# Softmax mixture on one core: evictions that gather column halves into row pairs on two engines, 32 KB store rows, and last stores in two queues

## The chip, the core and the metric

The kernel runs on one core of a Trainium2 chip. TensorE (PE), VectorE (DVE), ScalarE (ACT) and GpSimd (POOL) each take their own instructions in order. SyncE (SP) and ScalarE issue the DMAs here. SP's go to the queue that the profile calls q1, ScalarE's to q10. All of them run on the core's 16 DMA engines. The metric is the device time of one execution in microseconds; less is better.

## What is computed

For each of 32 x 128 = 4096 rows there are four heads of 4096 logits and four prior logits. The result is the mean of the four softmaxes, weighted with the softmax of the priors:

```python
prior_probs = np.exp(prior - prior.max(axis=-1, keepdims=True))
prior_probs = prior_probs / prior_probs.sum(axis=-1, keepdims=True)
softmax = np.exp(logits - logits.max(axis=-1, keepdims=True))
softmax = softmax / softmax.sum(axis=-1, keepdims=True)
mixture = np.sum(prior_probs[..., None] * softmax, axis=2)   # [32, 128, 4096]
```

The logits are 268.4 MB of float32, read once; the result is 67.1 MB, written once.

## The kernel before

**Tiling.** The 4096 rows are cut into G = 32 groups of 128, and each group into J = 2 tiles of M = 64 rows; row 2m + j of a group is row m of its tile j. So there are N = 64 tiles. A tile lies in a slot of 128 partitions: partition 2m + q holds the heads 2q and 2q + 1 of row m, 32 KB in all. Index i (0 or 1) names the half of a slot, one head per partition, 4096 numbers. There are five slots, and `load(n)` fills one with a 4 MB DMA from SP (line 65; the last tile comes in two halves, line 68).

**Work on a tile.** `top(n, i)` takes the row maximum on VectorE (line 74) and the exponential on ScalarE, in place, with its sum beside it (line 77). `weigh(n, i)` takes the reciprocal of the sum (line 82, VectorE), makes from it and the prior a 128 x 64 weight matrix (line 84, GpSimd), and multiplies with it on TensorE (line 91): the matmul adds the two partitions of a row, and the second call (i = 1) adds the other two heads in PSUM. A tile's 64 x 4096 results stand in one PSUM tile `acc` of 128 x 2048: partitions 0 to 63 hold columns 0 to 2047 (c = 0), partitions 64 to 127 columns 2048 to 4095 (c = 1). [...]

**Eviction and store.** `evict(n)` is one ScalarE copy of 128 x 2048 out of `acc` (line 106) into the group's place in the output buffer `obuf`, which has room for two groups. `store(g)` writes a group with two DMAs of 1 MB (line 111), one per column half c: 64 partitions, two rows j each, 8 KB per row. For groups below HOLD = 28 they are issued from ScalarE, right behind the eviction. The last four groups are held back: groups 28 and 29 stay in `obuf`, groups 30 and 31 go into a slot that is no longer needed, and all of them are stored from SP, behind the last loads in SP's queue.

**Order.** The order is written by hand. Step n of the loop (lines 148 to 163) issues, with w = n - 1: `top(n, 0)`, `weigh(w, 1)`, `load(w + 5)`, `top(n, 1)`, `weigh(n, 0)`, `evict(w)` and, for the second tile of a group, its store. So on VectorE a step is maximum, reciprocal, maximum, reciprocal; on ScalarE it is exponential, exponential, eviction of the tile before, sometimes a store. After the loop the last tile is finished (lines 165 to 169). Semaphores between engines are put in by the layer that records the program, from the tiles that instructions read and write; an instruction that waits holds up all that stands behind it on its engine.

Of the kernel before, what the change touches and what calls it, by code (L numbers as in the profile page):

```python
# [1 line left out]

# [4 lines left out]

FP32 = mybir.dt.float32
AF = mybir.ActivationFunctionType
ALU = mybir.AluOpType  # L10
AX = mybir.AxisListType

P = 128
M = 64
J = 2
Q = 2
BANK = 512
SLOTS = 5


@with_exitstack
def kernel(
    ctx: ExitStack,
    tc: tile.TileContext,
    logits: bass.AP,
    prior: bass.AP,
    out: bass.AP,
):
    nc = tc.nc
    B, S, H, V = logits.shape  # L30
    R = M * J
    G = B * S // R
    N = G * J
    W = V // 2
    assert G * R == B * S and G == 32 and H == 2 * Q and V == 8 * BANK


    lg = logits.rearrange("b s h v -> (b s) h v").rearrange(
        "(g m j) (q i) v -> g j m q (i v)", m=M, j=J, i=Q
    )  # L40
    ov = out.rearrange("b s v -> (b s) v").rearrange("(g m j) v -> g m j v", m=M, j=J)
    pv = prior.rearrange("b s h -> (b s) h").rearrange("(g r) h -> g r h", r=R)

    cpool = ctx.enter_context(tc.tile_pool(name="cpool", bufs=1))
    psum = ctx.enter_context(tc.tile_pool(name="psum", bufs=1, space=bass.MemoryType.PSUM))

    slots = [cpool.tile([P, Q, V], FP32, name=f"slot{i}") for i in range(SLOTS)]

    obuf = cpool.tile([P, 2, J, W], FP32, name="obuf")
    accs = [psum.tile([P, W], FP32, name=f"acc{i}") for i in range(2)]  # L50

    sel = cpool.tile([P, M], FP32, name="sel")
    wts = [[cpool.tile([P, M], FP32, name=f"wt{k}{i}") for i in range(Q)] for k in range(2)]
    pr = cpool.tile([G, R, H], FP32, name="pr")
    pn = cpool.tile([G, J, Q, M, Q], FP32, name="pn")
    pmax = cpool.tile([G, R], FP32, name="pmax")
    pp = cpool.tile([P, J, Q, G], FP32, name="pp")
    nmax = [cpool.tile([P, N], FP32, name=f"nmax{i}") for i in range(Q)]
    dsum = [cpool.tile([P, N], FP32, name=f"dsum{i}") for i in range(Q)]
    rden = [cpool.tile([P, N], FP32, name=f"rden{i}") for i in range(Q)]  # L60

    def load(n):
        src = lg[n // J, n % J]
        if n < N - 1:
            nc.sync.dma_start(out=slots[n % SLOTS], in_=src)  # L65
        else:
            for i in range(Q):
                nc.sync.dma_start(
                    out=slots[n % SLOTS][:, i], in_=src[:, :, i * V : (i + 1) * V]
                )  # L70

    def top(n, i):
        x = slots[n % SLOTS][:, i]
        nc.vector.tensor_reduce(  # L74
            out=nmax[i][:, n : n + 1], in_=x, axis=AX.X, op=ALU.max, negate=True
        )
        nc.scalar.activation(  # L77
            x, x, AF.Exp, bias=nmax[i][:, n : n + 1], accum_out=dsum[i][:, n : n + 1]
        )

    def weigh(n, i):
        nc.vector.reciprocal(rden[i][:, n : n + 1], dsum[i][:, n : n + 1])  # L82
        wt = wts[n % 2][i]
        nc.gpsimd.tensor_scalar(  # L84
            out=wt, in0=sel, scalar1=rden[i][:, n : n + 1],
            scalar2=pp[:, n % J, i, n // J : n // J + 1], op0=ALU.mult, op1=ALU.mult,
        )

        for b in range(W // BANK):
            for c in range(2):  # L90
                nc.tensor.matmul(  # L91
                    accs[n % 2][c * M : (c + 1) * M, b * BANK : (b + 1) * BANK],
                    lhsT=wt,
                    rhs=slots[n % SLOTS][:, i, c * W + b * BANK : c * W + (b + 1) * BANK],
                    start=i == 0, stop=i == Q - 1,
                )

    HOLD = G - 4

    def home(g):  # L100
        if g < G - 2:
            return obuf[:, g % 2]
        return slots[(N - 5) % SLOTS][:, g % 2].rearrange("p (j w) -> p j w", j=J)

    def evict(n):
        nc.scalar.copy(home(n // J)[:, n % J], accs[n % 2])  # L106

    def store(g, js=slice(0, J)):
        eng = nc.scalar if g < HOLD else nc.sync
        for c in range(2):  # L110
            eng.dma_start(
                out=ov[g, :, js, c * W : (c + 1) * W], in_=home(g)[c * M : (c + 1) * M, js]
            )

    with tc.manual_schedule():
        for n in range(SLOTS):
            load(n)
        nc.scalar.dma_start(out=pr, in_=pv)

        nc.gpsimd.memset(sel, 1.0)  # L120
        nc.gpsimd.affine_select(  # L121
            out=sel, in_=sel, compare_op=ALU.is_ge, fill=0.0, base=0,
            pattern=[[-Q, M]], channel_multiplier=1,
        )
        nc.gpsimd.affine_select(  # L125
            out=sel, in_=sel, compare_op=ALU.is_ge, fill=0.0, base=Q - 1,
            pattern=[[Q, M]], channel_multiplier=-1,
        )

        nc.vector.reduce_max(pmax, pr, axis=AX.X)  # L130
        nc.vector.tensor_sub(pr, pr, pmax.unsqueeze(2).to_broadcast([G, R, H]))  # L131
        nc.scalar.activation(pr, pr, AF.Exp)  # L132
        nc.vector.reduce_sum(pmax, pr, axis=AX.X)  # L133
        nc.vector.reciprocal(pmax, pmax)  # L134
        prv = pr.rearrange("g (m j) (q i) -> g j i m q", j=J, i=Q)
        pmv = pmax.rearrange("g (m j) -> g j m", j=J)
        for j in range(J):
            for i in range(Q):
                nc.vector.tensor_mul(  # L139
                    pn[:, j, i], prv[:, j, i], pmv[:, j].unsqueeze(2).to_broadcast([G, M, Q])  # L140
                )
        pq = pn.rearrange("g j i m q -> g j i (m q)")
        for t in range(P // 32):
            nc.vector.transpose(  # L144
                pp[32 * t : 32 * (t + 1)], pq[:, :, :, 32 * t : 32 * (t + 1)]
            )

        for n in range(N):
            w = n - 1
            top(n, 0)  # L150
            if w >= 0:
                weigh(w, 1)
                if w + SLOTS < N:
                    load(w + SLOTS)
            top(n, 1)
            weigh(n, 0)
            if w >= 0:
                evict(w)
                if w == N - SLOTS:
                    for g in range(HOLD, w // J):  # L160
                        store(g)
                if w % J == J - 1 and (w // J < HOLD or w >= N - SLOTS):
                    store(w // J)

        n = N - 1
        store(n // J, slice(0, 1))
        weigh(n, 1)
        evict(n)
        store(n // J, slice(1, 2))


# [1 line left out]
_INS = ['logits', 'prior']  # L173
_OUTS = [((32, 128, 4096), 'float32')]


# [23 lines left out]
```

## Time and profile before

| | |
|---|---|
| median of 3 runs | 794.33 us (794.04 to 794.41) |
| the profiled execution | 794.6 us |
| its span on the page | 792.9 us |
| busy: PE, DVE, ACT, POOL | 69%, 72%, 76%, 6% |
| moved by DMA | 335.95 MB, 424 GB/s over the span |
| mean granted TensorE clock | 0.877 of full speed |

The span runs from the first to the last instruction of the program that the profiler recorded; 1.7 us of the execution lie outside it. A row of the timeline gives start, duration, engine, line, operation, output, input and shape; in brackets stands how long the engine had been idle before and what ended that. A start is counted from the beginning of the span. The next instruction of an engine can start up to 0.1 us before the record of the one before it ends.

### The profile page before, as it was taken

How to read it: one execution, taken by the hardware profiler on the slowest of the kernel's cores; microseconds unless marked ns; L12 is line 12 of the kernel's file. 1: busy time of each engine (PE TensorE's matmuls, PEld its weight loads, DVE VectorE, ACT ScalarE, POOL GpSimd, SP SyncE). 2: the span in 40 equal slices, each digit the busy share in tenths (PEclk: the TensorE clock that was granted, in tenths of full speed). 3: DMA queues.
4: the chain of work that ended last, by engine and by line, in shares of the span. 5: the costliest groups of instructions: out<-in, count | busy, mean ns of one | idle time of the engine just before them, and what ended most of it. 6: DMA issues, size and time to landing. Idle time of an engine off the chain costs nothing.

```text
span 792.9 us, 5418 instructions
## 1 busy us (share of the span) xinstructions
PE 544.3 (69%) x2048; PEld 159.6 (20%) x2048; DVE 573.3 (72%) x268; ACT 600.1 (76%) x322; POOL 51.1 (6%) x135
## 2 busy tenths in 40 slices
PE   0766567687776687666866677768568687776773
PEld 0212112122221122121211221212112122222221
DVE  5986867767768668677687686776866867767890
ACT  1897777787787787777877778778778777787893
POOL 0000000000000000000000000000000000000000
PEclk9998998877898977999799899887998877998998
DMA  9999999999999999999999999999999999999997
GB/s 375 441 414 431 430 426 429 433 431 428 433 436 433 434 434 431 429 427 437 429 431 429 431 434 431 433 436 430 433 432 432 427 432 427 432 431 438 432 386 234
DMA packets 18681, 335.95 MB, mean 424 GB/s; under 512 B 2112, under 2 KB 2112, under 8 KB 2144
## 3 DMA queue, kind: packets, MB, share of 16 engines
q1 hardware_dynamic: 10544, 276.83, 81.9%
q10 hardware_dynamic: 8112, 58.79, 17.6%
q8 instruction: 16, 0.26, 0.1%
q14 instruction: 9, 0.07, 0.0%
HBM read 268.50 MB, written 67.11 MB: 423 GB/s over the span
## 4 chain that ended last, share of the span: by engine, by line
DMA 76%; PE 10%; DVE 10%; issue 1%; POOL 1%; ACT 1%; SPq 0%; POOLq 0%
DMA slot<-in_logits_dram 76%; PE acc L91 10%; DVE nmax L74 9%; POOL wt L84 1%; ACT slot L77 0%; ACT slot L106 0%; SPq L65 0%; DVE rden L82 0%; POOLq L84 0%
## 5 line engine op out<-in xcount | busy, mean ns | idle before, releaser
L91 PE MATMUL acc<-slot,wt 128*64 128x512 f32 x2048 | 544.3, 689 | 236.6 <-POOL wt L84 236.5
L74 DVE TENSOR_REDUCE nmax<-slot 128x1 f32<-128x4096 f32 x128 | 563.5, 4410 | 194.6 <-DMA slot<-in_logits_dram 194.6
L77 ACT ACTIVATE slot<-slot,nmax 128x4096 f32<-128x4096 f32 x128 | 474.6, 3708 | 177.1 <-DVE nmax L74 175.7
L91 PEld LDWEIGHTS acc<-slot,wt 128*64 128x64 f32 x2048 | 159.6, 157 | 620.4 <-POOL wt L84 315.4
L106 ACT COPY obuf<-acc 128x2048 f32<-128x2048 f32 x60 | 110.7, 1845 | 0.0
L84 POOL TENSOR_SCALAR wt<-sel,rden,pp 128x64 f32<-128x64 f32 x128 | 50.3, 393 | 725.3 <-DVE rden L82 725.3
L77 ACT ACTIVATION_READ_ACCUMULATOR slot<-slot,nmax 128x1 f32 x128 | 23.9, 187 | 0.0
L82 DVE RECIPROCAL rden<-dsum 128x1 f32<-128x1 f32 x128 | 19.6, 153 | 5.1 <-ACT slot L77 5.1
L106 ACT COPY slot<-acc 128x2048 f32<-128x2048 f32 x4 | 7.4, 1850 | 2.8 <-PE acc L91 2.8
L130 DVE TENSOR_REDUCE pmax<-pr 32x128 f32<-32x512 f32 x1 | 0.7, 673 | 2.7 <-DMA pr<-in_prior_dram 2.7
L132 ACT ACT_TABLE_LOAD x1 | 1.3, 1283 | 1.2 <-PEq L184 1.2
L132 ACT ACTIVATE pr<-pr 32x512 f32<-32x512 f32 x1 | 0.6, 629 | 1.6 <-DVE pr L131 1.6
L144 DVE STREAM_TRANSPOSE pp<-pn 32x128 f32<-32x128 f32 x4 | 1.2, 302 | 0.1
L133 DVE TENSOR_REDUCE pmax<-pr 32x128 f32<-32x512 f32 x1 | 0.7, 674 | 0.7 <-ACT pr L132 0.7
L134 DVE RECIPROCAL pmax<-pmax 32x128 f32<-32x128 f32 x1 | 0.9, 941 | 0.0
L139 DVE TENSOR_TENSOR pn<-pr,pmax 32x128 f32<-32x128 f32 x4 | 0.9, 274 | 0.0
L131 DVE TENSOR_TENSOR pr<-pr,pmax 32x512 f32<-32x512 f32 x1 | 0.7, 678 | 0.0
L121 POOL TENSOR_SCALAR_AFFINE_SELECT sel<-sel 128x64 f32<-128x64 f32 x1 | 0.2, 238 | 0.1
L125 POOL TENSOR_SCALAR_AFFINE_SELECT sel<-sel 128x64 f32<-128x64 f32 x1 | 0.2, 238 | 0.1
L120 POOL MEMSET sel<- 128x64 f32 x1 | 0.2, 151 | 0.3 <-POOLq L184 0.3
L184 POOL MEMSET const-float32-0.0<- 128x1 f32 x1 | 0.1, 98 | 0.3 <-issue 0.3
L184 POOL MEMSET const-bfloat16-1.0<- 128x1 bf16 x1 | 0.1, 101 | 0.0
(2 smaller groups left out, 0.2 us busy)
## 6 DMA issues: line engine op xcount, KB each, us to landing
slot<-in_logits_dram SPq DMA_DIRECT2D x63, 4096.0 KB, 38.0
out_dram<-obuf ACTq DMA_DIRECT2D x56, 1024.0 KB, 25.5
slot<-in_logits_dram SPq DMA_DIRECT2D x2, 2048.0 KB, 32.9
out_dram<-obuf SPq DMA_DIRECT2D x4, 1024.0 KB, 31.0
out_dram<-slot SPq DMA_DIRECT2D x2, 1024.0 KB, 15.5
out_dram<-slot SPq DMA_DIRECT2D x4, 512.0 KB, 9.2
pr<-in_prior_dram ACTq DMA_DIRECT2D x1, 64.0 KB, 1.8
```

What stands on the lines that cost most here:

```text
L74: nc.vector.tensor_reduce(out=nmax[i][:, n : n + 1], in_=x, axis=AX.X, op=ALU.max, negate=True)
L77: nc.scalar.activation(x, x, AF.Exp, bias=nmax[i][:, n : n + 1], accum_out=dsum[i][:, n : n + 1])
L82: nc.vector.reciprocal(rden[i][:, n : n + 1], dsum[i][:, n : n + 1])
L84: nc.gpsimd.tensor_scalar(out=wt, in0=sel, scalar1=rden[i][:, n : n + 1], scalar2=pp[:, n % J, i, n // J : n // J + 1], op0=ALU.mult, op1= ...
L91: nc.tensor.matmul(accs[n % 2][c * M : (c + 1) * M, b * BANK : (b + 1) * BANK], lhsT=wt, rhs=slots[n % SLOTS][:, i, c * W + b * BANK : c * ...
L106: nc.scalar.copy(home(n // J)[:, n % J], accs[n % 2])
L130: nc.vector.reduce_max(pmax, pr, axis=AX.X)
L131: nc.vector.tensor_sub(pr, pr, pmax.unsqueeze(2).to_broadcast([G, R, H]))
L132: nc.scalar.activation(pr, pr, AF.Exp)
L134: nc.vector.reciprocal(pmax, pmax)
L139: nc.vector.tensor_mul(pn[:, j, i], prv[:, j, i], pmv[:, j].unsqueeze(2).to_broadcast([G, M, Q]))
L144: nc.vector.transpose(pp[32 * t : 32 * (t + 1)], pq[:, :, :, 32 * t : 32 * (t + 1)])
```

## The change

In groups below 28, `evict` now makes four copies of 64 partitions instead of one of 128. For each column half c, ScalarE copies columns 0 to 1535 of that half (`CUT` = 3 banks) and VectorE the last 512 (the fourth bank). Both halves go to the same 64 partitions of `obuf`, so that a partition holds whole rows: 2 rows x 4096 columns, 32 KB, which also lie together in the result. Even groups use partitions 0 to 63, odd ones 64 to 127. `obuf` keeps its size. VectorE's two copies stand at the end of its step, behind the second reciprocal and ahead of the next step's first maximum. `store` becomes a single DMA of 2 MB from ScalarE with 64 runs of 32 KB.

The last four groups are evicted as before by ScalarE alone, in the old layout, and stored in parts: column half 0 (partitions 0 to 63) from SP, column half 1 (partitions 64 to 127) from ScalarE. Groups 28 and 29 now lie in slot 3, groups 30 and 31 in `obuf`. So the last six tiles use slots 4, 0, 1, 2, 4, 0, and each of their loads is issued one step later than before, four steps ahead instead of five. ScalarE issues its parts of groups 28 and 29 in step 62, between the two exponentials. The very last tile is evicted and stored in two halves of 1024 columns.

```diff
+CUT = 3 * BANK
...
-    obuf = cpool.tile([P, 2, J, W], FP32, name="obuf")
+    obuf = cpool.tile([P, J, V], FP32, name="obuf")
...
+    def slot(n):
+        return slots[n % SLOTS if n < N - 6 else (4, 0, 1, 2)[(n - N + 6) % 4]]
...
+    def part(eng, g, c, js=slice(0, J), lo=0, hi=W):
+        eng.dma_start(
+            out=ov[g, :, js, c * W + lo : c * W + hi],
+            in_=home(g)[c * M : (c + 1) * M, js, lo:hi],
+        )
...
     def home(g):
-        if g < G - 2:
-            return obuf[:, g % 2]
-        return slots[(N - 5) % SLOTS][:, g % 2].rearrange("p (j w) -> p j w", j=J)
-
-    def evict(n):
-        nc.scalar.copy(home(n // J)[:, n % J], accs[n % 2])
-
-    def store(g, js=slice(0, J)):
-        eng = nc.scalar if g < HOLD else nc.sync
+        if g < HOLD:
+            return obuf[(g % 2) * M : (g % 2 + 1) * M]
+        x = slots[3] if g < G - 2 else obuf
+        return x[:, g % 2].rearrange("p (j w) -> p j w", j=J)
+
+    def evict(n, lo=0, hi=W):
+        acc = accs[n % 2]
+        dst = home(n // J)[:, n % J]
+        if n // J >= HOLD:
+            nc.scalar.copy(dst[:, lo:hi], acc[:, lo:hi])
+            return
         for c in range(2):
-            eng.dma_start(
-                out=ov[g, :, js, c * W : (c + 1) * W], in_=home(g)[c * M : (c + 1) * M, js]
+            nc.scalar.copy(dst[:, c * W : c * W + CUT], acc[c * M : (c + 1) * M, :CUT])
+        for c in range(2):
+            nc.vector.tensor_copy(
+                dst[:, c * W + CUT : (c + 1) * W], acc[c * M : (c + 1) * M, CUT:]
             )
+
+    def store(g):
+        nc.scalar.dma_start(out=ov[g], in_=home(g))
...
             top(n, 0)
+            if n == N - 2:
+                for g in (HOLD, HOLD + 1):
+                    part(nc.scalar, g, 1)
             if w >= 0:
                 weigh(w, 1)
-                if w + SLOTS < N:
-                    load(w + SLOTS)
+                for k in range(SLOTS, N):
+                    if prior_user(k) == w:
+                        load(k)
+                if w == N - 3:
+                    for g in (HOLD, HOLD + 1):
+                        part(nc.sync, g, 0)
             top(n, 1)
             weigh(n, 0)
             if w >= 0:
                 evict(w)
-                if w == N - SLOTS:
-                    for g in range(HOLD, w // J):
-                        store(g)
-                if w % J == J - 1 and (w // J < HOLD or w >= N - SLOTS):
-                    store(w // J)
+                g = w // J
+                if w % J == J - 1 and g < HOLD:
+                    store(g)
+                elif w == N - 3 or w == N - 2:
+                    js = slice(0, J) if w == N - 3 else slice(0, 1)
+                    part(nc.sync, g, 0, js)
+                    part(nc.scalar, g, 1, js)
 
         n = N - 1
-        store(n // J, slice(0, 1))
         weigh(n, 1)
-        evict(n)
-        store(n // J, slice(1, 2))
+        for lo in (0, W // 2):
+            evict(n, lo, lo + W // 2)
+            part(nc.sync, n // J, 0, slice(1, 2), lo, lo + W // 2)
+            part(nc.scalar, n // J, 1, slice(1, 2), lo, lo + W // 2)
```

`prior_user(k)` gives the last tile before k that uses the same slot. The lines of the changed kernel that come up later: maxima at 77, exponentials at 80, reciprocals at 85, ScalarE's copies at 123 (groups below 28) and 120 (the last four), VectorE's copies at 125, stores at 130 and 102.

## Prediction, made before the changed kernel ran

> **What bounds the kernel now.** I read the page's 40 slices first, then its chain, then the timeline of one step in the middle.
>
> ```profile
> DMA  9999999999999999999999999999999999999997
> GB/s 375 441 414 431 430 426 429 433 431 428 433 436 433 434 434 431 429 427 437 429 431 429 431 434 431 433 436 430 433 432 432 427 432 427 432 431 438 432 386 234
> ...
> DMA 76%; PE 10%; DVE 10%; issue 1%; POOL 1%; ACT 1%; SPq 0%; POOLq 0%
> ...
> L74 DVE TENSOR_REDUCE nmax<-slot 128x1 f32<-128x4096 f32 x128 | 563.5, 4410 | 194.6 <-DMA slot<-in_logits_dram 194.6
> ```
>
> The 16 DMA engines are busy from end to end at some 430 GB/s, in all but the last two slices; 76% of the chain is loads; and VectorE, which takes the maximum first, was idle 194.6 us for loads. So a step lasts as long as its share of the traffic. Two stretches of the timeline show the step with all its slack (VectorE, then ScalarE):
>
> ```profile
> 321.62 4.42 DVE L74 TENSOR_REDUCE nmax<-slot 128x1 f32<-128x4096 f32 x1 [3.24 <-DMA slot<-in_logits_dram]
> 325.96 0.15 DVE L82 RECIPROCAL rden<-dsum 128x1 f32<-128x1 f32 x1
> 326.03 4.40 DVE L74 TENSOR_REDUCE nmax<-slot 128x1 f32<-128x4096 f32 x1
> 330.35 0.15 DVE L82 RECIPROCAL rden<-dsum 128x1 f32<-128x1 f32 x1
> 333.76 4.42 DVE L74 TENSOR_REDUCE nmax<-slot 128x1 f32<-128x4096 f32 x1 [3.26 <-DMA slot<-in_logits_dram]
> ```
>
> ```profile
> 326.08 3.71 ACT L77 ACTIVATE slot<-slot,nmax 128x4096 f32<-128x4096 f32 x1 [2.18 <-DVE nmax L74]
> 329.69 0.19 ACT L77 ACTIVATION_READ_ACCUMULATOR slot<-slot,nmax 128x1 f32 x1
> 330.46 3.71 ACT L77 ACTIVATE slot<-slot,nmax 128x4096 f32<-128x4096 f32 x1 [0.58 <-DVE nmax L74]
> 334.08 0.19 ACT L77 ACTIVATION_READ_ACCUMULATOR slot<-slot,nmax 128x1 f32 x1
> 334.17 1.84 ACT L106 COPY obuf<-acc 128x2048 f32<-128x2048 f32 x1
> ```
>
> Count from the first maximum (321.62). VectorE is done after 8.9 us and idle until 12.14, the step's length. ScalarE runs about half a step behind: exponentials at +4.46 and +8.84, eviction at +12.55, when VectorE is already in the next step. Nobody waits for that late eviction. This offset decides the case.
>
> **Evictions, groups 0 to 27.** Counted as busy time they are cheap. ScalarE copies: the page's 128x4096 ACTIVATE takes 3.708 us and the 32x512 one 0.629, so 0.859 ns per column; 1536 columns are 512 fewer than the 1.845 us copy, so 1.40 us each, two of them 2.70 with the 0.10 overlap of ScalarE's rows. Bounds: 1.38 (three quarters of 1.845) and 1.845 (no less than the whole copy); I take 1.40, since the two ACTIVATE rows differ almost in proportion to their columns. VectorE's 512 columns out of PSUM: no row of before shows VectorE reading PSUM. The nearest rows are its 32x512 operations, 0.67 to 0.68 us; by the slope between the 32x512 and the 128x4096 reduction (1.04 ns per column) 0.53 is the least, and one RECIPROCAL of 0.94 over fewer columns is the most. I take 0.67, as the size agrees: two are 1.26 us with VectorE's 0.08 overlap. Side by side, both engines would fit into 12.14 us: VectorE 8.9 + 1.3, ScalarE 7.7 + 2.7 + 0.3.
>
> They do not run side by side. In the order of the built program with its waits, VectorE's step reads:
>
> ```text
> 20 L77 TensorReduce nmax_79<-slot_63 128x1
> 21 L85 Reciprocal rden_82<-dsum_80 128x1 [waits Activation_49]
> 22 L125 TensorCopy obuf<-acc_68 64x512 [waits PE_49,Activation_49]
> 23 L125 TensorCopy obuf<-acc_68 64x512
> 24 L77 TensorReduce nmax_78<-slot_64 128x1 [waits DMAHW4_49]
> 25 L85 Reciprocal rden_83<-dsum_81 128x1
> ```
>
> Row 22 waits for TensorE, as it must, and for ScalarE. How far ScalarE must have come is seen in row 25: that reciprocal needs the step's second exponential, yet waits no more, so row 22 waited at least that far; and the semaphore count in row 22 is the one ScalarE reaches behind both its copies. So the first VectorE copy starts after ScalarE's last one, and behind it on VectorE stands the next maximum, for which all of the next step waits.
>
> [...]
>
> The new step, on VectorE: ScalarE's first copy at +12.55 (it follows the exponential directly; TensorE is done before +9), both done at +15.25; 0.03 us of signal (the last exponential's end at 772.69 to the reciprocal at 772.72); VectorE's copies until +16.54; next maximum at **+16.46** (overlap 0.08). VectorE thus waits some 6.4 us per step for ScalarE, and the loads have 4.3 us of slack per step: 16.46 us against 12.14 of traffic. Loads, issued four or five steps ahead, then never bind.
>
> This holds for steps 1 to 56 (evictions of tiles 0 to 55). Step 1 starts at 23.22, when the second load lands, as before. Step 57 starts at 23.22 + 56 x 16.46 = 945.0.
>
> **Stores.** A group's store is one issue instead of two (0.6 us less on ScalarE, inside slack). Whatever 32 KB runs from 64 partitions cost or save, DMAs now have room: 336 MB in 1000 us. I cost it at nothing; without that cover see the second rival. ScalarE's store waits for VectorE's copies, +16.54, and ScalarE's next work is at +16.46 + 4.46: hidden.
>
> **The last seven steps.** Evictions are ScalarE's alone. Loads are in, so ScalarE paces: from the first exponential of step 62 (759.18) to that of step 63 (768.89) it is 9.71 us, and with VectorE ahead 3.70 + 3.69 + 1.75 = 9.15. First exponential of step 57 at 945.0 + 4.46 = 949.5; six steps 9.71 + 5 x 9.15 = 55.5; three DMA issues ahead of ScalarE's work in step 62, 0.6 each, 1.8. So step 63's first exponential is at 1006.8. From there to the last eviction it was 780.92 - 768.89 = 12.0, giving 1018.8 (ScalarE's issue there hides in 2.79 us of idle time). Two half copies (0.97 each) with an issue (0.6) between: 1021.4. Last store: 1.8 us (the 64 KB prior load, issue to landing), 1.2 for 512 KB at 430 GB/s, an issue of 0.5: 1024.9. About 1 us to the end: span 1026. With the 1.7 us outside: **1028 us**. The sum is against the profiled 794.6, 0.3 above the median; that is nothing here.
>
> Moving loads one step later and slots about costs nothing: no load binds. The split of the last stores saves at the end what the backlog cost. Now 9.6 us pass from the last store's issue (783.3) to the end; then about 4.
>
> [...] Windows of 4 us late in the run of before:
>
> ```profile
> 768.00:772.00 4.00, 3.50 (x16) 1.06 (x16) 4.00 (x1) 4.00 (x2) 0.39 (x1) 1.00 1.00 342
> 784.00:788.00 4.00, 0.00 (x0) 0.00 (x0) 0.00 (x0) 0.00 (x0) 0.00 (x0) 0.74 0.98 279
> ```
>
> The last three columns are clock, DMA share, GB/s: stores of one partition half each keep the engines busy (1.00, 0.98) yet move only 342 and 279 GB/s. [...]
>
> **Rivals.** (1) *The wait costs nothing and the copies overlap* (not slower). Then steps stay at 12.14 us of traffic and the end shortens by 9.6 - 4: 789 us. It decides if VectorE's copies start near +9 instead of +15.3. For it: both engines' busy time fits. Against it: the wait in row 22. (2) *They overlap, but stores from half the partitions in long runs drag.* 28 stores of 2.1 MB at 300 GB/s (between the windows' 279 and 342) instead of 430 cost 58.7 MB x (1/300 - 1/430) = 59 us at most, where stores run alone; with loads between, half: about 820. (3) *The wait holds and copies cost as much as the whole one*, 1.845 each: 0.9 us x 56 = 50 more, 1078. The 64 partitions, moved across halves, are in no row of before.
>
> **Chances.** Forecast 0.82, rival 1 0.05, rival 2 0.04, rival 3 (1056 and more) 0.09. The forecast's bounds: with 1.38 and 0.53 us the step is 16.1, 20 us less, 1008; half of rival 3's surcharge gives 1056. The range 1008 to 1056 leaves out the rivals. A measurement of this kernel tells about 0.2% from no change: faster 0.05, same 0.01, slower 0.94.
>
> **What would show it.** Right: VectorE's idle time before line 125, released by ScalarE's line 123, near 56 x 6.4 = 360 us; hardly any waiting for loads at line 77; maxima 16.5 us apart; DMA share in the middle near 12.1/16.5 = 0.74. Wrong: line 125 starting while line 123 runs, or maxima still led by loads. The number, not the mechanism, fails if copies differ from 1.40 and 0.67: 0.1 us per step is 5.6 us.

## The result, and the profile after

The changed kernel takes **1055.51 us** (median of 4 runs, 1055.23 to 1055.63) against 794.18 us (793.97 to 794.41) beside it: a ratio of 1.3287, 95% interval 1.327 to 1.3305. It is slower by a third. The time lies 27.5 us above the predicted one and inside the range, 0.5 us below its upper end. The profiled execution has a span of 1053.7 us. The medians and ranges of the experiments below leave out two executions that took over 1.5% longer than the fastest of the same kernel (846.51 us of `e2_own_bank_tile`, 842.83 us of `e4_scalar_alone`).

The page of the changed kernel, the same rows as shown of before (busy, mean ns, then idle time before and what ended it):

```profile
DMA  9999778877797779887797779877797779857998
GB/s 398 432 412 372 306 292 340 313 305 287 291 368 284 296 309 337 326 307 284 279 378 277 300 289 349 308 306 282 299 363 289 285 293 365 309 169 276 378 410 291
...
L77 DVE TENSOR_REDUCE nmax<-slot 128x1 f32<-128x4096 f32 x128 | 563.0, 4405 | 6.9 <-DMA slot<-in_logits_dram 6.0
...
L125 DVE COPY obuf<-acc 64x512 f32<-64x512 f32 x112 | 77.1, 689 | 376.8 <-ACT obuf L123 375.1
L123 ACT COPY obuf<-acc 64x1536 f32<-64x1536 f32 x112 | 160.4, 1432 | 2.0
```

VectorE's wait for loads has gone from 194.6 us to 6.0. In its place stand 375.1 us of VectorE's copies waiting for ScalarE's: 6.7 us in each of 56 steps. The DMA engines, full before, have gaps from the fifth slice on. Two stretches of the timeline show how a step runs now (VectorE, then ScalarE):

```profile
497.98 4.42 DVE L77 TENSOR_REDUCE nmax<-slot 128x1 f32<-128x4096 f32 x1
...
506.70 0.15 DVE L85 RECIPROCAL rden<-dsum 128x1 f32<-128x1 f32 x1
513.56 1.41 DVE L125 COPY obuf<-acc 64x512 f32<-64x512 f32 x2 [6.70 <-ACT obuf L123]
514.88 4.41 DVE L77 TENSOR_REDUCE nmax<-slot 128x1 f32<-128x4096 f32 x1
```

```profile
510.43 0.19 ACT L80 ACTIVATION_READ_ACCUMULATOR slot<-slot,nmax 128x1 f32 x1
510.65 2.88 ACT L123 COPY obuf<-acc 64x1536 f32<-64x1536 f32 x2
519.33 3.71 ACT L80 ACTIVATE slot<-slot,nmax 128x4096 f32<-128x4096 f32 x1 [5.80 <-DVE nmax L77]
```

Each engine now waits for the other once per step: VectorE 6.70 us for the copies, then ScalarE 5.80 us for the maximum that stood behind VectorE's copies.

### The profile page after: what moved, and what is told of

Read it like the earlier page. It is cut to its first block, busy times and chain, and to the rows that moved or that the text cites. A ratio compares the mean times of both kernels' runs of the same rounds, so it can differ in the third digit from the quotient of the medians.

```text
span 1053.7 us, 5689 instructions
## 1 busy us (share of the span) xinstructions
PE 581.2 (55%) x2048; PEld 168.9 (16%) x2048; DVE 647.7 (61%) x380; ACT 662.1 (63%) x379; POOL 51.1 (5%) x135
## 3 DMA queue, kind: packets, MB, share of 16 engines
q10 hardware_dynamic: 2960, 62.98, 17.3%
## 5 line engine op out<-in xcount | busy, mean ns | idle before, releaser
L94 PE MATMUL acc<-slot,wt 128*64 128x512 f32 x2048 | 581.2, 731 | 464.4 <-POOL wt L87 464.3
L94 PEld LDWEIGHTS acc<-slot,wt 128*64 128x64 f32 x2048 | 168.9, 168 | 875.9 <-POOL wt L87 528.7
L125 DVE COPY obuf<-acc 64x512 f32<-64x512 f32 x112 | 77.1, 689 | 376.8 <-ACT obuf L123 375.1
L123 ACT COPY obuf<-acc 64x1536 f32<-64x1536 f32 x112 | 160.4, 1432 | 2.0
L120 ACT COPY obuf<-acc 128x2048 f32<-128x2048 f32 (+1 forms) x5 | 7.6, 1515 | 3.4 <-PE acc L94 2.8
```

What stands on the lines that cost most here:

```text
L94: nc.tensor.matmul(accs[n % 2][c * M : (c + 1) * M, b * BANK : (b + 1) * BANK], lhsT=wt, rhs=slot(n)[:, i, c * W + b * BANK : c * W + (b + ...
L120: nc.scalar.copy(dst[:, lo:hi], acc[:, lo:hi])
L123: nc.scalar.copy(dst[:, c * W : c * W + CUT], acc[c * M : (c + 1) * M, :CUT])
L125: nc.vector.tensor_copy(dst[:, c * W + CUT : (c + 1) * W], acc[c * M : (c + 1) * M, CUT:])
```

## The experiments

All ratios are to the kernel before, run on the same chip. The theory, called T below: the wait of VectorE's copies for ScalarE's costs all of it. Rivals: the gathering copies (the four copies of an eviction) are dear by themselves; or stores in 32 KB runs from half the partitions drag, that is, hold up the loads.

### 1 to 4: take the wait away

Four versions of the changed kernel, each without the full wait. `e1_vector_first` exchanges the two loops, so that VectorE's copies are recorded first:

```diff
-        for c in range(2):
-            nc.scalar.copy(dst[:, c * W : c * W + CUT], acc[c * M : (c + 1) * M, :CUT])
         for c in range(2):
             nc.vector.tensor_copy(
                 dst[:, c * W + CUT : (c + 1) * W], acc[c * M : (c + 1) * M, CUT:]
             )
+        for c in range(2):
+            nc.scalar.copy(dst[:, c * W : c * W + CUT], acc[c * M : (c + 1) * M, :CUT])
```

> The changed kernel with the two copy loops of the eviction in the other order: VectorE's copies are recorded first, ScalarE's second, so the wait now points the other way, from ScalarE to VectorE. Theory (VectorE stands 6.7 us per step behind ScalarE's copies, and the next maximum behind it): VectorE copies at about +9 of the step, ScalarE's find them done at +12.7 and wait for nothing; the step falls from 16.9 us back to the 12.14 us of the traffic, and the time to 787 to 796 us. VectorE's wait for ScalarE at its copies, 375 us, disappears. Rival (the four copies by themselves, or the 32 KB stores from half the partitions, are what costs): the step stays above 14 us and the time above 850 us.

`e2_own_bank_tile` keeps the order and gives VectorE's bank a PSUM tile of its own:

```diff
-    accs = [psum.tile([P, W], FP32, name=f"acc{i}") for i in range(2)]
+    accs = [psum.tile([P, CUT], FP32, name=f"acc{i}") for i in range(2)]
+    last = [psum.tile([P, BANK], FP32, name=f"last{i}") for i in range(2)]
...
-                dst[:, c * W + CUT : (c + 1) * W], acc[c * M : (c + 1) * M, CUT:]
+                dst[:, c * W + CUT : (c + 1) * W], last[n % 2][c * M : (c + 1) * M, :]
```

> The changed kernel with the fourth PSUM bank, which VectorE reads, in a PSUM tile of its own; order and copies as in the changed kernel, but for the last four groups, where ScalarE needs two copies for a tile. In the order of the built program VectorE's copies then wait for TensorE alone. Theory (the wait was put in because both engines read one PSUM tile, and it is the whole cost): as with the other order of the loops, 787 to 797 us; the last seven steps some 0.1 to 0.2 us longer each. Rival (two engines reading PSUM at a time hold each other up): VectorE's copy well over 0.69 us, or ScalarE's over 1.43.

`e3_one_step_late` lets VectorE copy one step later, behind the next step's first maximum, with the store behind it (`evict_rest` makes VectorE's two copies):

```diff
...
             top(n, 0)
+            if n >= 2 and (n - 2) // J < HOLD:
+                evict_rest(n - 2)
+                if n % J == J - 1:
+                    store((n - 2) // J)
...
```

> The changed kernel with VectorE's two copies issued behind the next step's first maximum instead of ahead of it, and the store behind them. The wait for ScalarE's copies stays in the program. Theory (what counts is what stands behind the waiting instruction on VectorE): the first maximum is no longer held up, but the second still is. The loop is then second maximum 4.40, second exponential 3.83, ScalarE's copies 2.88, VectorE's copies 1.41, some 0.07 between: 12.6 us per step instead of 16.9, against 12.14 of traffic; 56 steps by 0.45 us more than traffic gives some 812 to 820 us. Rival (the wait itself is the price, wherever it stands): still some 6 us per step, above 1000 us.

`e4_scalar_alone` lets ScalarE copy both halves whole, 64 x 2048 each, and VectorE nothing:

```diff
-            nc.scalar.copy(dst[:, c * W : c * W + CUT], acc[c * M : (c + 1) * M, :CUT])
-        for c in range(2):
-            nc.vector.tensor_copy(
-                dst[:, c * W + CUT : (c + 1) * W], acc[c * M : (c + 1) * M, CUT:]
-            )
+            nc.scalar.copy(dst[:, c * W : (c + 1) * W], acc[c * M : (c + 1) * M, :])
```

> The changed kernel with both column halves copied by ScalarE alone, 64 x 2048 each; VectorE copies nothing. Stores as in the changed kernel. Theory (nothing but VectorE's wait costs): ScalarE needs about 7.6 + 3.7 + 0.3 us per step, which fits into 12.14 us, so the traffic binds again: 787 to 797 us, and VectorE waits for loads again. Rival (32 KB stores from half the partitions drag): above 800 us, with DMA busy from end to end and fewer GB/s in the middle slices than the 430 of before.

Measured:

| | us, median (range) | ratio, 95% interval |
|---|---|---|
| `e1_vector_first` | 832.81 (830.86 to 834.32) | 1.0483 (1.0467 to 1.0498) |
| `e2_own_bank_tile` | 833.75 (832.47 to 837.21) | 1.0503 (1.0484 to 1.0522) |
| `e3_one_step_late` | 827.4 (826.23 to 829.66) | 1.0423 (1.0407 to 1.0439) |
| `e4_scalar_alone` | 834.13 (828.14 to 835.03) | 1.0488 (1.0464 to 1.0513) |

Recording the same four copies in another order takes 1055.51 - 832.81 = 223 us off. So the wait is the cause of most of the loss. It comes from the shared PSUM tile: with a tile of its own (`e2_own_bank_tile`) VectorE waits for TensorE instead of ScalarE, as this line of its page shows.

```profile
L131 DVE COPY obuf<-last 64x512 f32<-64x512 f32 x112 | 77.1, 688 | 85.8 <-PE last L96 83.6
```

In this run the two engines now and then read PSUM at the same time. From 132.77 us on ScalarE's copies run beside the last 0.47 us of VectorE's (131.83 to 133.24 us), and the pairs of copies take 2.88 and 1.41 us, as in the changed kernel. More overlap than such half microseconds was not found, so the run tells little of what two engines reading PSUM at a time cost each other.

But T fails on the rest: the first was expected at 787 to 796, and none of the four came near that; the third, expected at 812 to 820 for steps of 12.6 us, took 827. The four differ in who copies what and when, and lie within 8 us of each other. Something else costs 33 to 40 us, and the same with and without VectorE's copies. From the page of `e1_vector_first`:

```profile
DMA  9999999999999999999999999999999999999998
GB/s 381 432 425 419 411 432 422 410 416 423 411 413 420 400 412 425 408 416 421 409 413 423 406 402 425 397 428 405 418 408 408 418 424 393 358 342 420 391 327 241
...
L127 ACT COPY obuf<-acc 64x1536 f32<-64x1536 f32 x112 | 160.4, 1432 | 7.5 <-DVE obuf L123 3.2
L123 DVE COPY obuf<-acc 64x512 f32<-64x512 f32 x112 | 77.1, 688 | 88.9 <-PE acc L94 86.7
```

The copies cost what they cost in the changed kernel (1432 and 688 ns) and hardly wait for each other; the DMA engines are busy throughout, as before, yet move some 413 GB/s where they moved 431. That is the second rival. It was tested next; the changed end was tested too.

### 5: the changed end alone

`e5_new_end_only` is the kernel before with the changed kernel's slots, loads and stores of the last four groups; evictions and stores of the others are as before.

```diff
+    def slot(n):
+        return slots[n % SLOTS if n < N - 6 else (4, 0, 1, 2)[(n - N + 6) % 4]]
...
+                elif w == N - 3 or w == N - 2:
+                    js = slice(0, J) if w == N - 3 else slice(0, 1)
+                    part(nc.sync, g, 0, js)
+                    part(nc.scalar, g, 1, js)
```

> The kernel before with the changed end alone: slots of the last six tiles, held groups stored in two queues, the last tile evicted and stored in halves; evictions and stores of groups 0 to 27 as before. Theory of the first rival of the prediction: the last store leaves some 9.6 us before the end in the kernel before, and would leave it some 4 to 5 us before: 788 to 790 us. Rival (two queues move the halves no faster, as the 258 to 262 GB/s late in the run with VectorE's copies first suggest; ScalarE's three extra issues stand on its path): the end stays as long as it was, 793 to 797 us.

Measured: 792.66 (791.13 to 792.83), ratio 0.997 (0.9959 to 0.9982). A gain of 1.8 us: less than the 788 to 790 expected from the prediction's step, more than nothing. Windows of `e5_new_end_only`, same columns as in the prediction (the last three are clock, DMA share, GB/s):

```profile
768.00:772.00 4.00, 3.65 (x16) 1.06 (x16) 3.84 (x1) 3.29 (x2) 0.12 (x1) 1.00 1.00 395
...
776.00:780.00 4.00, 4.00 (x16) 1.31 (x14) 0.17 (x1) 2.61 (x3) 0.40 (x1) 0.74 0.75 258
```

The backlog of held stores does go out faster, 395 GB/s where it was 342. Behind the last copy only 5.7 us pass to the end of the span (791.1 - 785.45), where it was 10.1 (792.9 - 782.79). But that copy also ends 2.7 us later, and in between the engines have less to move (share 0.75): the last tile's arithmetic sets the end. Of the 2.7 us, 0.7 are the copy itself, which in two halves with an issue between takes 2.61 us instead of 1.87. The other 1.9 are seen in TensorE's last matmuls, before and in `e5_new_end_only`:

```profile
773.53 7.34 PE L91 MATMUL acc<-slot,wt 128*64 128x512 f32 x32 [1.38 <-POOL wt L84]
```

```profile
774.01 8.78 PE L93 MATMUL acc<-slot,wt 128*64 128x512 f32 x32 [2.19 <-POOL wt L86]
```

They start 0.5 us later, as ScalarE's last exponential does (773.07 instead of 772.59; ScalarE issues stores among its work), and take 1.4 us longer, at a granted clock of 0.83 and 0.74 in the windows from 772 to 780 us, where it was 1.00 before. The lower clock need not come with the changed end: in `e11_half_8k_runs` below, which has the same end, the clock is 1.00 in these windows and the 32 matmuls take 7.35 us. Two of the six executions of `e5_new_end_only` took 1.5 us less than the others (791.1 and 791.3, against 792.6 to 792.8), which would fit a full clock there, but they have no profile.

### 6 to 8: 16 KB runs, and which partitions

Three versions of the kernel before in which only the DMA of groups 0 to 29 differs: one DMA of 128 runs of 16 KB. `e6_rows_128_partitions` reads all partitions once, `e7_low_64_partitions` reads 0 to 63 twice, `e8_middle_64_partitions` 32 to 95 twice. The last two differ in the one number `lo`, 0 or 32; this is their edit:

```diff
     def store(g, js=slice(0, J)):
         eng = nc.scalar if g < HOLD else nc.sync
+        if g < G - 2:
+            x = home(g)[lo : lo + M].rearrange("p j w -> p (j w)")
+            eng.dma_start(out=ov[g], in_=x.unsqueeze(1).to_broadcast([M, J, V]))
+            return
```

> The kernel before; groups 0 to 29 are stored by one 2 MB DMA from all 128 partitions in runs of 16 KB, so that the columns of a group land in the wrong rows (same bytes, other places); evictions and all else as before. It tells whether longer runs drag by themselves. [...] Rival (long runs of stores as such, or their bursts, hold up the loads): 810 us and more.

> As the run with 128 partitions, but each store reads partitions 0 to 63 only, each partition's 16 KB twice, again in 16 KB runs to the same places (the result is wrong: half of it is missing, the rest doubled). Same bytes, same runs, same engines; only the source partitions differ. Theory (half the partitions): drag, held groups stored at about 260 to 340 GB/s, between the kernel before and the four runs above, 800 to 835 us. Rival (run length alone): the same time as with 128 partitions.

> As the run with partitions 0 to 63, but partitions 32 to 95 are read twice. [...] Theory B (64 partitions are too few, whichever they are): the same drag as with partitions 0 to 63. Rival (the writing side in HBM limits): all three alike.

Measured: 791.46 (ratio 0.9961, 0.9947 to 0.9974; the author's estimate was 786 to 795), 799.55 (1.0062, 1.0048 to 1.0076) and 791.32 (0.9959, 0.9943 to 0.9974). Windows of `e7_low_64_partitions`, then of `e8_middle_64_partitions`, where the held groups 28 and 29 are stored with the last loads in or nearly in:

```profile
764.00:768.00 4.00, 3.65 (x16) 1.06 (x16) 4.00 (x3) 4.00 (x3) 0.09 (x1) 1.00 1.08 274
768.00:772.00 4.00, 3.47 (x16) 1.06 (x16) 4.00 (x1) 4.00 (x2) 0.40 (x1) 1.00 0.95 197
772.00:776.00 4.00, 2.63 (x14) 0.92 (x14) 0.36 (x2) 4.00 (x3) 0.40 (x1) 1.00 0.98 203
```

```profile
764.00:768.00 4.00, 3.65 (x16) 1.06 (x16) 4.00 (x3) 4.00 (x3) 0.02 (x1) 1.00 1.00 426
768.00:772.00 4.00, 3.54 (x16) 1.06 (x16) 4.00 (x1) 4.00 (x2) 0.39 (x1) 1.00 0.97 395
772.00:776.00 4.00, 2.62 (x14) 0.91 (x14) 0.30 (x2) 4.00 (x3) 0.39 (x1) 1.00 1.02 344
```

In both the engines are busy (last but one column, 0.95 to 1.08). From 768 to 772 us they move 197 GB/s from partitions 0 to 63 and 395 from 32 to 95, with the same number of partitions, runs and bytes. So it is not the number of partitions but which ones; why, no run shows.

Beside loads, however, 16 KB runs from the low half cost nothing: from 300 to 420 us both runs move 432 GB/s, and the first maximum of the last tile starts at 763.41 us in `e7_low_64_partitions` and at 763.35 in `e8_middle_64_partitions`. The 8 us between them are lost in the end alone. What was left was the length of the runs.

### 9 and 10: 32 KB runs without the gathering

The kernel before, with the evictions going to a spare buffer, and one DMA of 64 runs of 32 KB per group from a buffer that nobody rewrites; `lo` is 0 in `e9_low_32k`, 32 in `e10_middle_32k`.

```diff
+        if g < G - 2:
+            eng.dma_start(out=ov[g], in_=obuf[lo:lo + M])
+            return
...
+        dst = spare if n // J < G - 2 else home(n // J)[:, n % J]
+        nc.scalar.copy(dst, accs[n % 2])
```

> The kernel before, except that groups 0 to 29 are each stored as one DMA of 64 runs of 32 KB that reads partitions 0 to 63 of a buffer that is never rewritten, while the evictions go to a spare buffer that nobody stores: the output is zero in these groups, and no gathering copies are made. [...] Rival (the loss in the gathering kernels came from their extra copies and waits, not from the stores): 790 to 802, the upper end for the two held groups stored slowly at the end.

> The same as the run with partitions 0 to 63, reading partitions 32 to 95 instead; output zero in groups 0 to 29 again. [...] Rival (long runs in few descriptors drag from any 64 partitions): within 5 us of the run with partitions 0 to 63.

Measured: 831.45 (829.7 to 837.55), ratio 1.0479 (1.0448 to 1.0509), against 792.88 (792.2 to 794.65), ratio 0.9982 (0.9974 to 0.9991). The author's estimates were 815 to 850 and 788 to 795. A window of 120 us in the middle, of `e9_low_32k` and of `e10_middle_32k`:

```profile
300.00:420.00 120.00, 82.63 (x310) 23.86 (x306) 81.39 (x37) 89.25 (x48) 7.43 (x19) 0.84 1.00 414
```

```profile
300.00:420.00 120.00, 80.01 (x316) 23.35 (x314) 88.76 (x40) 91.54 (x50) 7.87 (x20) 0.86 1.00 432
```

The 38 us are here without a single gathering copy, and they go away when the 64 partitions are others. In the same window the kernel before moved 432 GB/s and `e1_vector_first` 415. 4% of the 750 us or so in which loads and stores run together are some 32 us by these windows. In the profiled executions (837.55 us, the longest of its four, and 792.7) the first maximum of the last tile starts 29.7 us later, at 794.09 instead of 764.40. Another 15 us are lost behind it, and were not taken apart further.

### 11: the gathering with short runs

`e11_half_8k_runs` is `e1_vector_first` with each group stored by two DMAs of 8 KB runs from its one half of the partitions.

```diff
     def store(g):
-        nc.scalar.dma_start(out=ov[g], in_=home(g))
+        for c in range(2):
+            nc.scalar.dma_start(
+                out=ov[g, :, :, c * W : (c + 1) * W], in_=home(g)[:, :, c * W : (c + 1) * W]
+            )
```

> The changed kernel with VectorE's copies recorded first, and with each group below 28 stored from its one partition half by two DMAs of 8 KB runs instead of one of 32 KB runs; everything is computed. [...] Rival (any store from one half drags beside loads): 820 to 835, as with 32 KB runs.

Measured: **791.86** (791.69 to 793.15), ratio 0.997 (0.9958 to 0.9983); the author's estimate was 789 to 796. The same copies, the same partitions and bytes as in `e1_vector_first`, 41 us less. The result is that of the changed end alone (`e5_new_end_only`, also 0.997). So the gathering copies are free in this kernel once VectorE's don't wait for ScalarE's, and the drag is the long run from one half; how a long run holds up the loads was not shown. The copies are not without waits of their own: VectorE's wait 24.4 us in all, in 17 places, for earlier stores to leave `obuf`, but the DMA engines stay full and the time does not suffer. From its page:

```profile
GB/s 375 440 426 430 433 432 433 430 431 428 432 430 430 432 431 433 431 435 428 431 435 428 435 433 430 432 430 432 430 430 431 432 431 431 435 431 429 430 421 250
...
L127 ACT COPY obuf<-acc 64x1536 f32<-64x1536 f32 x112 | 160.5, 1433 | 8.3 <-issue 3.0
L123 DVE COPY obuf<-acc 64x512 f32<-64x512 f32 x112 | 77.1, 689 | 98.4 <-PE acc L94 72.2
```

### 12: a version meant to beat both

`e12_tile_per_half` maps rows so that a tile's gathered rows fill one half of the partitions and a group all 128.

```diff
-        "(g m j) (q i) v -> g j m q (i v)", m=M, j=J, i=Q
+        "(g j m) (q i) v -> g j m q (i v)", m=M, j=J, i=Q
...
+        if g >= G - 2:
+            nc.scalar.copy(home(g)[:, j, lo:hi], acc[:, lo:hi])
+            return
+        dst = home(g)[j * M : (j + 1) * M]
...
+        eng.dma_start(out=ov[g].rearrange("j m v -> (j m) v"), in_=home(g))
```

> A version meant to beat both: row j*64 + m of a group is row m of its tile j, so that a tile's gathered rows fill one partition half and the two tiles of a group fill all 128 partitions; groups 0 to 29 are gathered with VectorE's copies recorded first, and stored by one DMA of 128 runs of 16 KB; groups 30 and 31 keep the old layout and leave in halves from two queues; the last tile goes in two parts. Everything is computed. Theory (16 KB runs from all partitions cost 791.5 in the run that stored wrong rows so, and the two-queue end gave 1.8 alone; the two overlap in part): 788 to 791, at most 0.996 of the time before. Rival (the gathering copies and their waits cost something in the steady stage): 794 and more.

Measured: 794.28 (793.05 to 797.07), ratio 1.0007 (0.9996 to 1.0019). It missed. The middle runs at 430 GB/s like before; it loses behind that. These are VectorE's first maximum of each step and its copies there, without the other rows, in the profiled execution (796.8 us, one of the longer ones), and then first maxima of the kernel before:

```profile
724.75 4.42 DVE L75 TENSOR_REDUCE nmax<-slot 128x1 f32<-128x4096 f32 x1 [2.40 <-DMA slot<-in_logits_dram]
736.54 1.41 DVE L113 COPY obuf<-acc 64x512 f32<-64x512 f32 x2 [2.91 <-PE acc L92]
737.87 4.40 DVE L75 TENSOR_REDUCE nmax<-slot 128x1 f32<-128x4096 f32 x1
748.22 1.41 DVE L113 COPY obuf<-acc 64x512 f32<-64x512 f32 x2 [1.50 <-PE acc L92]
749.66 4.42 DVE L75 TENSOR_REDUCE nmax<-slot 128x1 f32<-128x4096 f32 x1
```

```profile
735.12 4.42 DVE L74 TENSOR_REDUCE nmax<-slot 128x1 f32<-128x4096 f32 x1 [2.91 <-DMA slot<-in_logits_dram]
744.88 4.42 DVE L74 TENSOR_REDUCE nmax<-slot 128x1 f32<-128x4096 f32 x1 [0.89 <-DMA slot<-in_logits_dram]
```

When stores are held back, only loads run, and a tile comes sooner: in the kernel before the last two of these steps are 735.12 - 723.33 = 11.8 and 744.88 - 735.12 = 9.8 us. With the gathering copies, which this version keeps up to group 29, they last 737.87 - 724.75 = 13.1 and 11.8 us, because VectorE's copies wait for TensorE and the next maximum stands behind them. The same maximum starts at 749.66 instead of 744.88. Of these 4.8 us the end gives 2.6 back (from that maximum to the end of the span 795.1 - 749.66 = 45.4 us, before 48.0). `e11_half_8k_runs`, which gathers only below group 28, starts it at 744.89, as before:

```profile
744.89 4.42 DVE L77 TENSOR_REDUCE nmax<-slot 128x1 f32<-128x4096 f32 x1 [0.84 <-DMA slot<-in_logits_dram]
```

That the two gathered groups are the cause is read from these rows; a version that gathers only 28 groups in this row order was not run. Of the versions that compute everything, `e5_new_end_only` and `e11_half_8k_runs` are the fastest, both 0.3% under before: what is gained is the end, and the gathering adds nothing to it.

## Why the prediction was right, and where its number was off

**The mechanism held.** The wait in row 22 of the built order was the one that decides: 375.1 us of VectorE's idle time (predicted near 360), loads no longer waited for (6.0 us), and 223 us gone when the same copies were recorded in another order. Rival 1 as it stood is refuted, since the copies did wait; rival 3 is refuted by the 64 x 1536 copy's 1.432 us.

That the time still fell inside the range was luck. 1055.51 lies 0.5 us below an upper end that was set at half of rival 3's surcharge, not worked out from what the terms below could come to: 0.01 us more per step would have passed it. (The lower end was 2 us too low by its own terms, as 1.38 and 0.53 us make a step of 16.14 us and a time of 1010; nothing hangs on it.)

**The mis-sized term is the step.** Predicted 16.46 us, in the timeline 514.88 - 497.98 = 16.90, and over all 56 steps (972.67 - 23.39) / 56 = 16.95. 0.49 x 56 = 27.4 us is the whole miss. Step 57, the first without such evictions, begins here:

```profile
972.67 4.42 DVE L77 TENSOR_REDUCE nmax<-slot 128x1 f32<-128x4096 f32 x1
```

The parts of the 0.49, from the rows shown above:
- ScalarE's first copy starts at +12.67, not +12.55: the copy of 128 partitions began before the record of the row ahead of it ended, the new one 0.03 us behind it.
- ScalarE's two copies take 2.88 us, not 2.70: 1.432 each instead of 1.40, and the 0.10 overlap assumed between them isn't there.
- VectorE's two take 1.41, not 1.26: 0.689 each instead of 0.67, and again no overlap between the two. The overlaps were taken from rows of other pairs of instructions, and did not carry over.
- The signal of 0.03 us was right (513.53 to 513.56), and so was the overlap of the next maximum with the copies' record, 0.09 instead of 0.08.

Of 0.49 these make the 0.44 of the step shown (16.90 - 16.46); the remaining 0.05 are steps longer than that one.

**The last seven steps** held in their sum: from step 57 to the end of the execution 83 us predicted, 1055.4 - 972.67 = 82.7 measured. Within it two errors of 0.8 us cancel: ScalarE's last copy ends 75.6 us into the stretch (1048.28 - 972.67) and not 76.4, and from there to the end of the span 5.4 us pass and not 4.6.

**Stores "cost at nothing"** was right for the time and wrong as a statement on the stores. The DMA share in the middle was expected at 0.74, and the two windows of 120 us from 300 to 540 give 0.84 and 0.81 at 319 and 306 GB/s, which is some 380 GB/s when busy, where it was 430 (the first of them):

```profile
300.00:420.00 120.00, 66.94 (x228) 19.26 (x226) 72.78 (x43) 74.66 (x43) 5.51 (x14) 0.74 0.84 319
```

The drag is there, and the wait's slack hides it. The queue rows show it too (packets, MB, share of the span), before and then after:

```profile
q10 hardware_dynamic: 8112, 58.79, 17.6%
```

```profile
q10 hardware_dynamic: 2960, 62.98, 17.3%
```

17.6% of 792.9 us for 58.79 MB are 2.37 us per MB; 17.3% of 1053.7 us for 62.98 MB are 2.89. So the prediction's second rival was a second mechanism under the first. Its price, 820, was near, as the versions without the wait took 827 to 834, but by luck: it was half of a bound, taken from 8 KB runs with no loads beside them, and 8 KB runs cost nothing beside loads (791.86 us in `e11_half_8k_runs`). What it lacked is that it matters which 64 partitions they are (831.45 us in `e9_low_32k`, 792.88 in `e10_middle_32k`).

**The changed end** was credited with some 5 us in rival 1's 789. It is worth 1.8. From the last store's issue to the end 5.6 us pass instead of 9.6 (4 were expected), but that issue comes 2.2 us later than before, at 785.49: the prediction left out that the last copy itself would end later.

On the rate, halves from two queues went out faster than halves one behind the other in one queue: from 768 to 772 us 395 GB/s in `e5_new_end_only` and 342 before (and 197 for the low half alone, in 16 KB runs, in `e7_low_64_partitions`). On the time of this kernel, 0.3%, there was little to gain.

## What to carry to other kernels

Before splitting an eviction between engines, look in the built order at what each copy waits for: copies of different columns of one PSUM tile may be recorded as dependent (375.1 us of waits here), and then the order of recording (832.81 us instead of 1055.51), or a tile of its own (833.75), decides; a wait at the end of an engine's step is paid with everything that stands behind it (6.70 us on VectorE, then 5.80 on ScalarE, in the step shown). Stores from partitions 0 to 63 alone are worth avoiding where nothing runs beside them (197 GB/s against 395; 64 to 127 alone were not measured), and 32 KB runs from one half also beside 32 KB loads (414 GB/s against 432); a slack elsewhere can hide that until it is removed. When a stage is bound by one resource, check the stages in which it is not: version 12 lost there.

## What the runs showed of the hardware that was not expected

- With no loads left, 64 partitions were stored at 395 GB/s or at 197, depending on whether they were 32 to 95 or 0 to 63 (`e8_middle_64_partitions` and `e7_low_64_partitions`, 768 to 772 us).
- Beside 32 KB loads, stores from one half of the partitions ran without loss in runs of 8 KB (432 GB/s in all, `e11_half_8k_runs`) and 16 KB (432, `e7_low_64_partitions`, up to its end), but not in runs of 32 KB (414 in `e9_low_32k`, 415 in `e1_vector_first`). The stores in long runs also went out faster beside the loads: one of 2 MB in 32 KB runs landed 16.6 us after its issue (`e1_vector_first`), those of 1 MB in 8 KB runs after 22.3 us (`e11_half_8k_runs`). So the long runs took a larger part of the traffic while they lasted: an estimate from these times is 2.1 MB in 16.6 us, some 126 GB/s, against 2.1 MB in 22.3 us, some 94, for two of the others side by side. What then limits the rate was not shown.
- A ScalarE copy out of PSUM took 1.845 us for 128 x 2048 (before) and 1.860 for 64 x 2048 (`e4_scalar_alone`): half the partitions cost as much.
